# A hybrid decoder layer on one NeuronCore: 8192 bytes of DMA scratch in place of 16384, longer buffers for split weights, and one set of weights 64 bytes into them

## The chip, the core and the metric

The kernel runs on one core of a Trainium2 chip. The core has a matrix engine (TensorE, PE in the profile), a vector engine (VectorE, DVE), an engine for activation functions (ScalarE, ACT), a general one (GpSimd, POOL) and a synchronizing one (SyncE, SP), which here only issues transfers. Each engine works through its own instructions in order; engines wait for one another by semaphores. Sixteen DMA engines move data between HBM and SBUF, the on-chip memory of 128 partitions. TensorE accumulates in PSUM, eight banks of 512 float32 per partition.

The metric is the device time of one execution in microseconds: the median of several, each on the chip.

## What is computed

One layer of a decoder for a prompt of 512 tokens and for eight samples of eight tokens each (64 tokens), which share the weights. The reference computes in float32; the parts that matter here, shortened:

```python
u = _rms(x) * g_pre_mix
proj = u @ w_in
z, xbc, dt_raw, q, k, v, ig, fg, og = jnp.split(proj, split_at, axis=-1)
xbc, conv_new = causal_conv(xbc, conv_buf, conv_w, conv_b)
...
y_ssd, h_new = ssd_scan(xs, dt, a, bm, cm, h_ssm)
...
h_ml, c_new, n_new, m_new = mlstm_scan(q, k, v, i_pre, logf, mc, mn, mm)
...
x = x + _rms(jnp.concatenate([y_ssd, h_ml], axis=-1) @ w_out) * g_post_mix
...
o = (attention of (u @ w_xq) over memory keys and values) @ w_xo
x = x + _rms(o) * g_post_x
u = _rms(x) * g_pre_ffn
x = x + _rms((jax.nn.silu(u @ w_gate) * (u @ w_up)) @ w_down) * g_post_ffn
```

The mixer is the first half: an SSD scan (Mamba-2) and an mLSTM side by side, both in chunks. `v` above are the mixer's values, the 1024 columns of `w_in` that the change is about.

## The kernel before

**Products in three parts.** A float32 product is made of three products of rounded numbers (type float32r): a weight `w` is split into `whi`, its rounding, and `wlo`, the rounded rest; an activation likewise into `uh` and `ul`. Then `whi*uh + whi*ul + wlo*uh` is accumulated in one PSUM bank (`gemm`, lines L202, L203 and L205). In most products the weights are the stationary operand, 128x128, and the activations move past them, 256, 288 or 320 columns at a time.

**Weights.** `split_w` loads 128 x 1024 weights into a buffer `raw` by SP's queue, casts them to `whi` on ScalarE (L180), and makes `wlo` by a subtraction on VectorE or GpSimd (L187). With `acc=True` part of `wlo` is made otherwise: ScalarE writes `-whi` (L184) and GpSimd issues a transfer that adds the weights from HBM onto it (L185). In the FFN the class `Seven` does the same for the tiles of its seven products (`low`, L1796 and L1797), and `cast` reads a part of the weights' `lo` back from HBM (L1557). All these transfers are issued by GpSimd; the others by SP, a few by ScalarE. The tags `whi` and `wlo` of the pool `weights` have three buffers each, which every stage of the kernel shares: `split_w`, the first two tiles `wi`, `cast`, and `high1`, `parts2` and `place3` of `Seven`.

**The mixer's values** (`values`, L801 on) are the other way round: for each of two halves `g` of the heads, four units of weights are the moving operand, 512 columns at a time, and the activations of a chunk of tokens are stationary (L815). They come by `split_w` with `cut=1024`, the whole of `wlo` on VectorE. Each product is placed behind a step of the SSD of the prompt (the list `steps_`), so that TensorE works on values while the SSD's chain runs on the other engines.

**Where tiles lie.** At the bottom of SBUF lies the scratch of the dynamic transfers. Behind it come the pools in the order of their creation: constants, `weights`, `newton`, `big` (large activations), and on top of these the pools of the single stages as a stack. Pools with `side="right"` are taken from the upper end downwards: `ssds` (the SSD of the samples, L681), `mls` (the mLSTM of the samples, L941), `big0` (L1035) and others. With `reuse_waits="tile"` a tile waits only for those earlier tiles whose bytes it takes. A tile of a right-hand pool can so wait for a tile of the stack on the left, where both reach the same bytes at different times.

**What sets the order.** The program is built with `schedule_with_timeline_sim=True`: outside of parts that are ordered by hand, a list scheduler with reckoned times sets the order on each engine when the program is built. Hand-written constraints (`issue_after`) bind it: `behind` and `split_behind` hold the projection's tiles of `z` back until given steps of the SSD (L1026), `steps_` the values. The FFN and the end of the attention are ordered by hand.

**Around the SSD's end.** For each pair of heads `ssd_prompt` builds decays in the tiles `lm` and `ec` and adds the part that comes from earlier chunks on GpSimd (L659, named `xs<-xs,ec` in the profile). Then the samples' mLSTM begins: `ds_` (L951 to L957), `qpad`, cleared on GpSimd (L959) and filled by eight products (L961), and `kws` (L967); then for each of eight batch elements its products L981 and L988 on TensorE. Its last products (L936) stand ahead of the output projection of the mixer (`out1`).

Of the kernel before, what the change touches and what calls it, by code (L numbers as in the profile page):

```python
# [12 lines left out]
F32R = mybir.dt.float32r  # L13
# [6 lines left out]
P = 128  # L20
# [87 lines left out]
CUT = 512  # L108
# [3 lines left out]
NWX = 3  # L112
# [3 lines left out]
def build(nc, tc, ctx, I, O):  # L116
# [4 lines left out]
    wp = ctx.enter_context(tc.tile_pool(name="weights", bufs=1))  # L121
# [14 lines left out]
    def GP(name="g"):  # L136
        return pg.tile([P, 512], F32, name=name, tag="g")
# [31 lines left out]

    loads, casts = [], []  # L170

    def split_w(src, n=1024, cut=CUT, acc=False, pool=None, to=None, raw=None):
        if raw is None:
            raw = wp.tile([P, 1024], F32, name="raw", tag="raw", bufs=2)
        loads.append(S.dma_start(raw[:, :n], src))
        if to:
            split(*to, raw[:, :n])
            return to
        hi, lo = [(pool or wp).tile([P, 1024], F32R, name=k, tag=k, bufs=NWX if pool else 3) for k in ("whi", "wlo")]
        casts.append(A.copy(hi[:, :n], raw[:, :n]))  # L180
        for e, a, b in ((V, 0, cut), (G, cut, n)):
            if b > a and e is G and acc:

                A.activation(lo[:, a:b], hi[:, a:b].bitcast(F32), AF.Copy, scale=-1.0)  # L184
                G.dma_start(lo[:, a:b], src[:, a:b], accum_op=ALU.add)  # L185
            elif b > a:
                e.tensor_tensor(lo[:, a:b], raw[:, a:b], hi[:, a:b].bitcast(F32), op=ALU.subtract)  # L187
        return hi, lo

    def split(hi, lo, src, eng=None, cast=None):  # L190
        c = (cast or A.copy)(hi, src)  # L191
        (eng or V).tensor_tensor(lo, src, hi.bitcast(F32), op=ALU.subtract)  # L192
        return c
# [109 lines left out]
        mm(psw[:, 0:256], wz[:, 0:128], wz, start=True, stop=True, skip_group_check=True)  # L303
    S.dma_start(par, I["par"])

    wi = [[wp.tile([P, 1024], F32R, name=k, tag=k, bufs=3) for k in ("whi", "wlo")] for _ in range(2)]
    raws = [wp.tile([P, 1024], F32, name="raw", tag="raw", bufs=2) for _ in range(2)]
    for k in range(KT):
        if k % 2 == 0:
# [32 lines left out]
    with tc.issue_after(uhk.ins), tc.issue_after(ulk.ins):  # L342
        w2 = split_w(I["win"][3], cut=1024, raw=sp.tile([P, 1024], F32, name="raw2"))
# [19 lines left out]
    with tc.issue_after(last[0].ins), tc.issue_after(last[1].ins):  # L363
        w3 = split_w(I["win"][4], cut=1024)
# [8 lines left out]
    def in_tile(i, evac, cut=CUT):  # L373

        if i < 5:
            for (t0, n), ps in zip(HALVES, ps0[i - 1]):
                if ps is None:
                    ps = GP("ps_in")[:, :n]
                    with tc.issue_after(rows[-1].ins):
                        gemm(ps, [(*w3, KT)], U, UL, t0, n)  # L380
                evac(t0, n, xs[:, 5 + i, t0:t0 + n] if i < 3 else ps)
        else:
            with tc.issue_after(pows[0].ins), tc.issue_after(rops[0].ins):
                with ExitStack() as after:
                    for m in split_behind.get(i, ()):
                        after.enter_context(tc.issue_after(m.ins))
                    w = split_w(I["win"][i], cut=cut, acc=True)
            if i in behind:
                gemm2([(*w, KT)], U, UL, evac, "ps_in", [0])
            with tc.issue_after(behind[i].ins) if i in behind else ExitStack():  # L390
                gemm2([(*w, KT)], U, UL, evac, "ps_in", [1] if i in behind else [0, 1])
# [310 lines left out]
    for g in range(2):  # L702
        for hb in range(2):
            dst = cpad[:, g, 4 * hb:4 * hb + 4, :].rearrange("p b t -> p (b t)")
            src = bc[:, 2 + g, TP + 32 * hb:TP + 32 * hb + 32]
# [4 lines left out]
    for g in range(2):  # L710
# [13 lines left out]
        for h in range(8):  # L724
            k, j = h % 2, (8 * g + h) // 2
# [75 lines left out]
    def values(g):  # L801


        units, banks = {}, {}

        def unit(u):
            units[u] = split_w(I["wv"][g][:, u, :], cut=1024)

        def product(ps, a, b, **kw):

            while steps_[0][0] <= done[0]:
                steps_.append(steps_.pop(0))
            done[0] += 1
            with tc.issue_after(steps_[-1][1].ins):
                mm(ps, a, b, skip_group_check=True, **kw)  # L815

        def products(u, c, first, last):
            (hi, lo), (t0, n) = units[u], CHUNKS[c]
            if first:
                banks[c] = GP("ps_v")  # L820
            ps = banks[c]
            for i in range(2):
                k, w = 2 * u + i, slice(512 * i, 512 * i + 512)
                s_, e_ = first and i == 0, last and i == 1
                if n == TS:

                    product(ps, U(k, t0, P), hi[:, w], start=s_, stop=e_)
                    product(ps[:n], U(k, t0, n), lo[:, w], start=False, stop=e_)
                else:
                    product(ps, U(k, t0, n), hi[:, w], start=s_, stop=False)  # L830
                    product(ps, UL(k, t0, n), hi[:, w], start=False, stop=False)
                    product(ps, U(k, t0, n), lo[:, w], start=False, stop=e_)
            if not last:
                return
            p2 = ps.rearrange("p (h k) -> p h k", h=2)
            if n == TS:
                o = vts[:TS, 2 * g:2 * g + 2, 0:256]
                A.copy(o, p2[TS:P])
                V.tensor_tensor(o, o, p2[:TS], op=ALU.add)
                A.activation(o, o, AF.Copy, scale=rx[:TS, 4:5])  # L840
            else:
                A.activation(vt4[:, c, 2 * g:2 * g + 2, 0:256], p2, AF.Copy, scale=rx[:, c:c + 1])

        for u in range(4):
            with tc.issue_after(added[0].ins) if g == 0 and u < 2 else ExitStack():
                unit(u)
            for c in range(3):
                products(u, c, u == 0, u == 3)
        for u in (1, 2, 3, 0):
            for c in (3, 4):  # L850
                products(u, c, u == 1, u == 0)
            if u == 1:
                unit(0)
# [35 lines left out]
    for h in range(4):  # L889
        q, k = qk[:, h, :], qk[:, 4 + h, :]  # L890
# [657 lines left out]

    def cast(key, src, low, pool=None):

        hi, lo = [(pool or wp).tile([P, 1024], F32R, name=k, tag=k, bufs=NWX if pool else 3) for k in ("whi", "wlo")]
        A.copy(hi, W[key])
        if low is None:
            A.activation(lo, W[key], AF.Copy, scale=-1.0)
            G.dma_start(lo, src, accum_op=ALU.add)
        else:
            G.dma_start(lo, pre[:, low, :])  # L1557
        W[key] = hi, lo
# [160 lines left out]
    for n_, (key, p) in enumerate(order):  # L1719
        src = I[{"xo": "wxo", "g": "wgate", "u": "wup"}[key[0]]][key[1]]  # L1720
        at_(order[n_ - 2][1] + 0.01 if n_ > 1 else -1, load, key, src)
        if key[1] == 3:
            at_(p, cast3, n_)
            at_((0.55, 1.05)[n_], low3, n_)
        else:
            at_(p, cast, key, src, PRE.index(key) if key in PRE else None, wx if key in (("g", 0), ("u", 0), ("g", 1)) else None)
# [43 lines left out]
    class Seven:  # L1770
# [26 lines left out]
                G.dma_start(out, src, accum_op=ALU.add)  # L1797

        def high1(s):
            s.h1 = wp.tile([P, 1024], F32R, name="whi", tag="whi", bufs=3)  # L1800
            s.c1 = A.copy(s.h1[:, s.all], s.r1[:, s.all])  # L1801

        def sums(s):
# [1 line left out]
            V.tensor_tensor(sw[:, s.LA], sw[:, s.LB], s.r1[:, s.LA], op=ALU.subtract)  # L1805

        def parts2(s):
            s.h2, s.l2 = [wp.tile([P, 1024], F32R, name=k, tag=k, bufs=3) for k in ("whi", "wlo")]
            split(s.h2[:, s.all], s.l2[:, s.all], sw[:, s.all])

        def diffs(s):
# [3 lines left out]
            V.tensor_tensor(s.d4[:, 0:s.n], s.r1[:, s.LB], sw[:, s.LA], op=ALU.subtract)  # L1815

        def place3(s):
            s.h3, s.l3 = [wp.tile([P, 1024], F32R, name=k, tag=k, bufs=3) for k in ("whi", "wlo")]
            s.low(s.l3[:, s.LA], s.r2[:, s.LB], s.src2[:, s.LB], s.made[1])

        def parts3(s):
# [524 lines left out]

# [10 lines left out]
```

## Time and profile before

| | us |
|---|---|
| median of three runs | 1094.43 (1092.6 to 1095.0) |
| the profiled execution, whole | 1092.51 |
| its span in the trace | 1090.7 |
| TensorE busy | 1081.4 |
| VectorE busy | 753.3 |
| ScalarE busy | 611.6 |
| GpSimd busy | 227.0 |

The mean granted clock of TensorE was 0.997 of full speed. In the profile, L12 is line 12 of the kernel. A row such as `L185 POOL DMA_DIRECT2D wlo<-win x32 | 27.9, 871 | 80.0 <-...` is a group of 32 instructions of line 185 on GpSimd that took 27.9 us in all and 871 ns each; the engine had been idle for 80.0 us just before them, and what follows the arrow ended that. A row of a timeline gives start, duration, engine, line, operation, tiles and count, and in brackets the idle time before it with its releaser. TensorE overlaps a matmul with the next, so the durations of single matmuls add up to more than the time they take. A queue row gives packets, megabytes and the share of 16 DMA engines' time.

### The profile page before, as it was taken

To read this page: it belongs to the slowest core of one execution; us is meant where nothing else is said; L and a number is where in the kernel's file an instruction comes from. 1 tells how busy PE (TensorE), PEld (TensorE's weight loads), DVE (VectorE), ACT (ScalarE), POOL (GpSimd) and SP (SyncE) were. 2 spreads that over 40 slices of the span, in tenths; PEclk is the share of its full clock that TensorE was granted. 3 is DMA by queue.
4 is the path that set the end of the run, shared out by engine and by line. 5 is a ranking of instruction groups with operands and counts; after the bars stand their busy time and mean duration, and the time that the engine had idled before them with its cause. 6 is when DMAs were issued, how large, how long until landed. Compare 5 with 4: busy or idle time off the path is not lost.

```text
span 1090.7 us, 20715 instructions
## 1 busy us (share of the span) xinstructions
PE 1081.4 (99%) x8124; PEld 1024.5 (94%) x8124; DVE 753.3 (69%) x1507; ACT 611.6 (56%) x1098; POOL 227.0 (21%) x305
## 2 busy tenths in 40 slices
PE   9999999999999999999999999999999999999997
PEld 8999887778999999999988879999999999999997
DVE  6896775758877775568644556666567887787555
ACT  7867622355654555656544445645567566656653
POOL 1332643313213111000144301100011121111000
PEclk9999999999999999999999999999999999999999
DMA  6785635435655448653467865644476687578532
GB/s 209 181 156 126 161 114 168 164 86 177 190 150 145 108 138 292 218 193 110 144 219 277 270 238 175 217 153 103 116 184 146 150 197 175 116 186 187 128 130 88
DMA packets 58966, 182.29 MB, mean 167 GB/s; under 512 B 6604, under 2 KB 11852, under 8 KB 58356
## 3 DMA queue, kind: packets, MB, share of 16 engines
q1 hardware_dynamic: 42740, 138.06, 38.7%
q0 software_dynamic: 15552, 41.95, 19.6%
q8 instruction: 64, 1.05, 0.4%
q10 hardware_dynamic: 576, 0.95, 0.2%
q14 instruction: 34, 0.28, 0.1%
HBM read 160.28 MB, written 20.65 MB: 166 GB/s over the span
## 4 chain that ended last, share of the span: by engine, by line
PE 90%; DVE 4%; DMA 2%; issue 2%; ACT 2%; POOL 0%; SPq 0%; DVEq 0%; ACTq 0%; POOLq 0%
PE ps_in L203 5%; PE ps_in L202 5%; PE ps_in L205 5%; PE ps_v L815 3%; PE ps_o L205 3%; PE ps_o L203 3%; PE ps_o L202 3%; PE ps_u L1850 3%; PE ps_g L1850 3%; PE ps_g L1849 3%; PE ps_u L1851 3%; PE ps_g L1851 3%; PE ps_u L1849 3%; PE ps_dn L1849 2%; PE ps_dn L1851 2%; PE ps_dn L1850 2%
## 5 line engine op out<-in xcount | busy, mean ns | idle before, releaser
L202 PE MATMUL ps_in<-uh,whi 128*128 128x320 f32 (+1 forms) x544 | 163.3, 300 | 0.1
L205 PE MATMUL ps_in<-uh,wlo 128*128 128x320 f32 (+1 forms) x544 | 162.7, 299 | 0.2 <-DMA wlo<-win 0.2
L203 PE MATMUL ps_in<-ul,whi 128*128 128x320 f32 (+1 forms) x544 | 162.2, 298 | 0.0
L180 ACT CAST whi<-raw 128x1024 fp32r<-128x1024 f32 (+1 forms) x104 | 105.2, 1013 | 95.6 <-PE ps_in L203 25.9
L187 DVE TENSOR_TENSOR wlo<-raw,whi 128x512 fp32r<-128x512 f32 (+1 forms) x96 | 96.3, 1005 | 66.6 <-ACT whi L180 65.9
L202 PEld LDWEIGHTS ps_in<-uh,whi 128*128 128x128 f32 x544 | 102.9, 189 | 3.0 <-issue 1.7
L205 PEld LDWEIGHTS ps_in<-uh,wlo 128*128 128x128 f32 x544 | 102.7, 189 | 1.4 <-DMA wlo<-win 0.4
L203 PEld LDWEIGHTS ps_in<-ul,whi 128*128 128x128 f32 x544 | 102.9, 189 | 0.6
L185 POOL DMA_DIRECT2D wlo<-win x32 | 27.9, 871 | 80.0 <-ACT wlo L184 70.2
L1850 PE MATMUL ps_g<-b,whi 128*128 128x288 f32 x144 | 42.5, 295 | 0.0
L1850 PE MATMUL ps_u<-b,whi 128*128 128x288 f32 x144 | 42.5, 296 | 0.0
L1849 PE MATMUL ps_g<-b,whi 128*128 128x288 f32 x144 | 42.4, 295 | 0.0
L1849 PE MATMUL ps_u<-b,whi 128*128 128x288 f32 x144 | 42.2, 294 | 0.0
L1822 ACT CAST whi<-rawx 128x1024 fp32r<-128x1024 f32 (+1 forms) x26 | 25.6, 985 | 27.8 <-PE ps_dn L1850 13.8
L192 DVE TENSOR_TENSOR wlo<-sw,whi 128x1024 fp32r<-128x1024 f32 (+1 forms) x26 | 29.6, 1140 | 14.9 <-ACT whi L191 14.8
L202 PE MATMUL ps_xo<-qh,whi 128*128 128x288 f32 x128 | 38.6, 302 | 0.2 <-ACT whi L180 0.2
L205 PE MATMUL ps_o<-mixm_h,wlo 128*128 128x256 f32 (+1 forms) x128 | 37.8, 296 | 0.0
L202 PE MATMUL ps_o<-mixs_h,whi 128*128 128x320 f32 (+1 forms) x128 | 37.7, 295 | 0.0
L202 PE MATMUL ps_xq<-u2h,whi 128*128 128x320 f32 (+1 forms) x128 | 37.7, 299 | 0.0
L1801 ACT CAST whi<-raw 128x1024 fp32r<-128x1024 f32 (+1 forms) x26 | 25.6, 984 | 21.6 <-PE ps_g L1850 9.6
L203 PE MATMUL ps_o<-mixm_l,whi 128*128 128x256 f32 (+1 forms) x128 | 37.7, 294 | 0.0
L203 PE MATMUL ps_xo<-ql,whi 128*128 128x288 f32 x128 | 37.6, 295 | 0.0
(765 smaller groups left out, 3848.6 us busy)
## 6 DMA issues: line engine op xcount, KB each, us to landing
raw<-win SPq DMA_DIRECT2D x35, 512.0 KB, 4.1
raw<-wout SPq DMA_DIRECT2D x17, 512.0 KB, 3.6
raw<-wxq SPq DMA_DIRECT2D x13, 512.0 KB, 3.6
raw<-wgate SPq DMA_DIRECT2D x13, 512.0 KB, 3.7
raw<-wup SPq DMA_DIRECT2D x13, 512.0 KB, 4.8
wlo<-win POOLq DMA_DIRECT2D x24, 256.0 KB, 5.1
kva<-kc SPq DMA_DIRECT2D x12, 512.0 KB, 5.8
kva<-vc SPq DMA_DIRECT2D x12, 512.0 KB, 6.5
```

The costliest lines, as they stand in the source:

```text
L180: casts.append(A.copy(hi[:, :n], raw[:, :n]))
L185: G.dma_start(lo[:, a:b], src[:, a:b], accum_op=ALU.add)
L187: e.tensor_tensor(lo[:, a:b], raw[:, a:b], hi[:, a:b].bitcast(F32), op=ALU.subtract)
L192: (eng or V).tensor_tensor(lo, src, hi.bitcast(F32), op=ALU.subtract)
L202: mm(ps, wh, ah, start=i == 0, stop=False)
L203: mm(ps, wh, al, start=False, stop=False)
L205: m = mm(ps, tiles[order[c]][1], xh(order[c], t0, n), start=False, stop=c == len(tiles) - 1)
L815: mm(ps, a, b, skip_group_check=True, **kw)
L1801: s.c1 = A.copy(s.h1[:, s.all], s.r1[:, s.all])
L1849: mm(ps, wh, b[0][k], start=start and k == 0, stop=False, skip_group_check=True)
L1850: mm(ps, wh, b[1][k], start=False, stop=False, skip_group_check=True)
L1851: m = mm(ps, wl, b[0][k], start=False, stop=k == nk - 1, skip_group_check=True)
```

## The change

Three edits. `kernel` asks for 8192 bytes per partition of scratch for dynamic transfers; before it took the default, 16384. A new helper `half_w` gives the buffers of split weights out: 1088 columns (4352 bytes) instead of 1024 (4096), of which the 1024 from column `o` on are used; every user of the tags `whi` and `wlo` of the pool `weights` takes its buffer from it. The mixer's values pass `o=16`, so their weights start 16 columns, 64 bytes, into the buffers; all others start at 0. `split_w` hands `o` on.

```diff
--- before.py
+++ after.py
@@ -169,14 +169,17 @@
 
     loads, casts = [], []
 
-    def split_w(src, n=1024, cut=CUT, acc=False, pool=None, to=None, raw=None):
+    def half_w(k, o=0):
+        return wp.tile([P, 1088], F32R, name=k, tag=k, bufs=3)[:, o:o + 1024]
+
+    def split_w(src, n=1024, cut=CUT, acc=False, pool=None, to=None, raw=None, o=0):
         if raw is None:
             raw = wp.tile([P, 1024], F32, name="raw", tag="raw", bufs=2)
         loads.append(S.dma_start(raw[:, :n], src))
         if to:
             split(*to, raw[:, :n])
             return to
-        hi, lo = [(pool or wp).tile([P, 1024], F32R, name=k, tag=k, bufs=NWX if pool else 3) for k in ("whi", "wlo")]
+        hi, lo = [pool.tile([P, 1024], F32R, name=k, tag=k, bufs=NWX) if pool else half_w(k, o) for k in ("whi", "wlo")]
         casts.append(A.copy(hi[:, :n], raw[:, :n]))
         for e, a, b in ((V, 0, cut), (G, cut, n)):
             if b > a and e is G and acc:
@@ -303,7 +306,7 @@
         mm(psw[:, 0:256], wz[:, 0:128], wz, start=True, stop=True, skip_group_check=True)
     S.dma_start(par, I["par"])
 
-    wi = [[wp.tile([P, 1024], F32R, name=k, tag=k, bufs=3) for k in ("whi", "wlo")] for _ in range(2)]
+    wi = [[half_w(k) for k in ("whi", "wlo")] for _ in range(2)]
     raws = [wp.tile([P, 1024], F32, name="raw", tag="raw", bufs=2) for _ in range(2)]
     for k in range(KT):
         if k % 2 == 0:
@@ -804,7 +807,7 @@
         units, banks = {}, {}
 
         def unit(u):
-            units[u] = split_w(I["wv"][g][:, u, :], cut=1024)
+            units[u] = split_w(I["wv"][g][:, u, :], cut=1024, o=16)
 
         def product(ps, a, b, **kw):
 
@@ -1548,7 +1551,7 @@
 
     def cast(key, src, low, pool=None):
 
-        hi, lo = [(pool or wp).tile([P, 1024], F32R, name=k, tag=k, bufs=NWX if pool else 3) for k in ("whi", "wlo")]
+        hi, lo = [pool.tile([P, 1024], F32R, name=k, tag=k, bufs=NWX) if pool else half_w(k) for k in ("whi", "wlo")]
         A.copy(hi, W[key])
         if low is None:
             A.activation(lo, W[key], AF.Copy, scale=-1.0)
@@ -1797,7 +1800,7 @@
                 G.dma_start(out, src, accum_op=ALU.add)
 
         def high1(s):
-            s.h1 = wp.tile([P, 1024], F32R, name="whi", tag="whi", bufs=3)
+            s.h1 = half_w("whi")
             s.c1 = A.copy(s.h1[:, s.all], s.r1[:, s.all])
 
         def sums(s):
@@ -1805,7 +1808,7 @@
             V.tensor_tensor(sw[:, s.LA], sw[:, s.LB], s.r1[:, s.LA], op=ALU.subtract)
 
         def parts2(s):
-            s.h2, s.l2 = [wp.tile([P, 1024], F32R, name=k, tag=k, bufs=3) for k in ("whi", "wlo")]
+            s.h2, s.l2 = [half_w(k) for k in ("whi", "wlo")]
             split(s.h2[:, s.all], s.l2[:, s.all], sw[:, s.all])
 
         def diffs(s):
@@ -1815,7 +1818,7 @@
             V.tensor_tensor(s.d4[:, 0:s.n], s.r1[:, s.LB], sw[:, s.LA], op=ALU.subtract)
 
         def place3(s):
-            s.h3, s.l3 = [wp.tile([P, 1024], F32R, name=k, tag=k, bufs=3) for k in ("whi", "wlo")]
+            s.h3, s.l3 = [half_w(k) for k in ("whi", "wlo")]
             s.low(s.l3[:, s.LA], s.r2[:, s.LB], s.src2[:, s.LB], s.made[1])
 
         def parts3(s):
@@ -2346,7 +2349,7 @@
 
 def kernel(**inputs):
     arrays = pack(inputs)
-    nc = bacc.Bacc("TRN2", target_bir_lowering=False, num_devices=1)
+    nc = bacc.Bacc("TRN2", target_bir_lowering=False, num_devices=1, dynamic_dma_scratch_size=8192)
     I = {k: nc.dram_tensor(k, v.shape, mybir.dt.from_np(v.dtype), kind="ExternalInput").ap() for k, v in arrays.items()}
     O = {k: nc.dram_tensor("o_" + k, s, F32, kind="ExternalOutput").ap() for k, s in OUTS.items()}
     with tile.TileContext(nc, **TCOPT) as tc:
```

## The prediction

> **What bounds the kernel now.** I read the page first, then the waits of TensorE, then the busy time of each engine by stage.
>
> ```profile
> PE 1081.4 (99%) x8124; PEld 1024.5 (94%) x8124; DVE 753.3 (69%) x1507; ACT 611.6 (56%) x1098; POOL 227.0 (21%) x305
> ...
> q0 software_dynamic: 15552, 41.95, 19.6%
> ...
> PE 90%; DVE 4%; DMA 2%; issue 2%; ACT 2%; POOL 0%; SPq 0%; DVEq 0%; ACTq 0%; POOLq 0%
> ```
>
> TensorE is busy for 1081.4 of 1090.7 us and holds 90% of the chain that ended last; what is left is mostly the start and the last stores. The waits of TensorE by releaser say the same:
>
> ```profile
> PE ps_warm L303 <- DVE wz L300: 1.1, 1, 1.1
> PE ps_ct L554 <- ACT r L533: 0.3, 1, 0.3
> PE ps_in L205 <- DMA wlo<-win: 0.2, 1, 0.2
> PE ps_xo L202 <- ACT whi L180: 0.2, 1, 0.2
> ```
>
> Four waits, 1.8 us in all. So the change can gain in three ways only: products that take less time, products that switch less between kinds, or one of these 0.2 us. It can lose wherever a transfer or another engine comes so late that TensorE has nothing to do. The places where that is near are those in which the change can alter the order of work, 206 to 264 us (columns: stretch, its length, then busy time of PE, PEld, DVE, ACT, POOL):
>
> ```profile
> 206.00:222.00 16.00, 16.00 (x88) 12.41 (x87) 11.65 (x20) 5.49 (x8) 1.93 (x1) 1.00 0.49 161
> 222.00:240.00 18.00, 18.00 (x99) 13.36 (x98) 7.94 (x20) 9.08 (x14) 3.37 (x4) 1.00 0.23 58
> 240.00:256.00 16.00, 15.76 (x137) 14.37 (x137) 12.38 (x30) 9.03 (x17) 4.15 (x7) 1.00 0.57 126
> 256.00:264.00 8.00, 8.00 (x63) 8.00 (x62) 7.94 (x18) 6.78 (x13) 6.41 (x13) 1.00 0.95 347
> ```
>
> TensorE is full there at a granted clock of 1.00, but from 256 to 264 us VectorE (7.94 of 8.00) and GpSimd (6.41) are full too.
>
> **The change part by part.** No instruction, byte or queue entry is added or taken out of the source. What changes is addresses, and through them which tile waits for which.
>
> **1. The values' weights, 64 bytes in.** These buffers are the moving operand of 224 products of 512 columns:
>
> ```profile
> L815 PE MATMUL ps_v<-whi,uh x80: 390/397/584, 167.0 to 239.6; 128*128 128x512 f32 x80
> ...
> L815 PE MATMUL ps_v<-wlo,uh x80: 387/394/582, 167.5 to 239.8; 128*128 128x512 f32 x64, 128*64 128x512 f32 x16
> ...
> L815 PE MATMUL ps_v<-whi,ul x64: 390/394/582, 167.3 to 238.5; 128*128 128x512 f32 x64
> ```
>
> Matmuls overlap, so a product's price is the distance from one start to the next, not its 394 ns:
>
> ```profile
> 174.51 0.39 PE L815 MATMUL ps_v<-wlo,uh 128*128 128x512 f32 x1
> ...
> 176.37 0.39 PE L815 MATMUL ps_v<-wlo,uh 128*128 128x512 f32 x1
> ```
>
> Eight intervals lie between these two: 1.86/8 = 232.5 ns each. Counting the tiles from the bottom of SBUF (16384 bytes of scratch, the constants, then the weights), each buffer of weights starts at 96 modulo 256 bytes now; 8192 less and 4352 in place of 4096 per buffer (both multiples of 256) leave that so, and only the values' weights go to 160. One other kind of product of this width has a moving operand that starts at 160 modulo 256, the attention's:
>
> ```profile
> 592.30 0.61 PE L1374 MATMUL ps_ov<-prh,mv 128*128 128x512 f32 x2
> 592.75 0.39 PE L1375 MATMUL ps_ov<-prl,mv 128*128 128x512 f32 x1
> ...
> 594.11 0.39 PE L1376 MATMUL ps_ov<-prh,mv 128*128 128x512 f32 x1
> ```
>
> From 592.30 to 594.11 there are again eight intervals (the first row holds two products): 226 ns. So the bounds are 0 and 224 x 6.5 ns = 1.5 us gained, if the phase of the address is the reason. The stationary operand and the accumulation differ between the two as well, so I take half, **-0.7 us**. Nothing hides it: TensorE is full in these rows' stretch.
>
> [...]
>
> The producers of these weights (the cast on ScalarE, the subtraction on VectorE, the load on SP's queue) keep their shapes, and none of the 1.8 us of waits lies on values, so they cost **0**.
>
> **2. Scratch halved.** [...] The queue's row has 15552 packets; they come from 108 issues (32 of L185, 52 of L1797, 24 for weights prepared ahead), 144 each. Issues by first and last start, with shortest, median and longest duration in ns:
>
> ```profile
> L185 POOL DMA_DIRECT2D wlo<-win x32 | 27.9, 871 | 80.0 <-ACT wlo L184 70.2
> ...
> L1797 POOL DMA_DIRECT2D wacc<-wgate x9: 850/850/932, 732.3 to 998.6; - x9
> ```
>
> The early issues take 871 ns on average, and the same kind between 732 and 999 us still 850. So with the large scratch an issue does not grow late in the run: no sign that space runs short. With half, the nearest row for a price is one more issue's length, 0.86 us, on the issues that come after the scratch is used up. What could be late is the transfer with the least room, in the FFN:
>
> ```profile
> 872.68 1.20 POOL L1797 DMA_DIRECT2D wlo<-wdown  x1
> ...
> wlo<-wdown POOLq DMA_DIRECT2D x8, 192.0 KB, 5.4
> ...
> 879.74 0.30 PE L1851 MATMUL ps_dn<-hh,wlo 128*128 128x288 f32 x1
> ```
>
> It is issued by 873.88, lands about 5.4 us on, 879.28, and TensorE wants it at 879.74: 0.46 us to spare. So 0.86 us more costs 0.4 us at this place, and there are two to six like it (eight such issues): 0.8 to 2.4 us. I take **0**, the lower end, since the flat 850 ns is the nearest row, and keep +2.4 for the range. Nothing can be gained here.
>
> [...]
>
> **3. Everything below moves.** The left side of SBUF starts 8192 bytes lower and its buffers of weights are 1536 bytes longer in all, so the tiles behind them sit 6656 bytes lower, while pools that allocate from the right stay. Two tiles of the samples' mLSTM, `qpad` and `ds_`, now share bytes with the prompt SSD's right-hand `lm` and `ec`; 6656 lower they don't. That takes away their wait for the last of the SSD. It shows in GpSimd's timeline:
>
> ```profile
> 222.00 1.01 POOL L659 TENSOR_TENSOR xs<-xs,ec 128x384 f32<-128x384 f32 x1 [14.08 <-DVE ec L657]
> 234.92 1.02 POOL L659 TENSOR_TENSOR xs<-xs,ec 128x384 f32<-128x384 f32 x1 [11.90 <-DVE ec L657]
> 236.98 0.88 POOL L185 DMA_DIRECT2D wlo<-win  x1 [1.03 <-ACT wlo L184]
> ...
> 255.22 1.00 POOL L659 TENSOR_TENSOR xs<-xs,ec 128x384 f32<-128x384 f32 x1 [0.45 <-DVE ec L657]
> 256.28 0.96 POOL L959 MEMSET qpad<- 128x1024 f32 x1
> ...
> 258.17 1.37 POOL L961 TENSOR_TENSOR qpad<-qk,vt 128x32 f32<-128x32 f32 x6
> 259.50 1.68 POOL L952 TENSOR_TENSOR ds__3156<-ds__3156,c 64x256 f32<-64x256 f32 x1
> 261.15 0.45 POOL L961 TENSOR_TENSOR qpad<-qk,vt 128x32 f32<-128x32 f32 x2
> ```
>
> The clearing of `qpad` starts right behind the last addition that reads `ec`, and this prologue (0.96 + 1.37 + 1.68 + 0.45 = 4.5 us) fills GpSimd where VectorE is full. Freed of the wait, the list scheduler, which fixes each engine's order when the program is built, may place it in the idle 14.08 or 11.90 us before the additions. Nothing on TensorE waits for the prologue today (no row in its waits), so an earlier one brings **0** by itself. It may change how the samples' products mix with the projection's, which has a price:
>
> ```profile
> 389.69 1.03 PE L936 MATMUL ps_ht<-c,num 128*128 128x128 f32 x8
> 390.49 0.37 PE L202 MATMUL ps_o<-mixs_h,whi 128*128 128x256 f32 x1
> 390.69 0.28 PE L203 MATMUL ps_o<-mixs_l,whi 128*128 128x256 f32 x1
> 390.81 0.27 PE L205 MATMUL ps_o<-mixs_h,wlo 128*128 128x256 f32 x1
> ```
>
> After plain products the first of the rounded ones takes 0.20 us to its successor, the next 0.12: 0.08 to 0.1 us for a switch. The mLSTM goes over 8 batch elements with some two switches each, so about 20 more or fewer are the most a new order makes: -2 to +2 us. With no reason for either sign I take **0**. An earlier prologue can also push work behind it; that is a rival.
>
> **Sum.** -0.7 + 0 + 0 = -0.7 us. The profiled execution took 1092.51 us, its span of 1090.7 and 1.8 around it; the sum against it gives 1091.8. The three runs (1092.6, 1094.43, 1095.0) have their median 1.9 us above it. The middle of all four is 1093.5, and **1092.8** follows. What a measurement of this kernel can tell from no change is about 0.2%, 2.2 us, the spread of the runs.
>
> **The rivals.**
>
> **Faster (1090.0).** The address is all of the 6.5 ns (-1.5), and the prologue, moved into GpSimd's idle 12 to 14 us, lets the scheduler join the samples' products into longer blocks (-2): 1093.5 - 3.5. For it: the idle stretches, and VectorE and GpSimd full from 256 to 264 us, a knot that would come undone. Against it: a full TensorE gains nothing from a knot elsewhere, and two other differences may explain the 6.5 ns.
>
> **Slower, a prologue in front of a load (1098.0).** GpSimd works in order. The issue at 236.98 is the very transfer for which TensorE waits 0.2 us already (`wlo<-win`), so it has no room. If the freed prologue is placed behind the addition at 234.92 and ahead of this issue, all of its 4.5 us appear on TensorE: 1093.5 + 4.5. It decides from the point where more than the 1.03 us of idle ahead of the issue is filled. Against it: the scheduler reckons times and has 11.90 us of room earlier; its inputs are there by 228 us, but its reckoned times need not be the chip's.
>
> **Slower, the scratch (1095.2).** As in step 2, with the upper end: 1092.8 + 2.4. For it: 108 issues through half the room. Against it: the duration that doesn't vary over the run.
>
> **It does nothing (1093.5).** The scheduler leaves the order as it is and the phase has no effect. It lies inside my forecast's own spread and is counted with it.
>
> **How the numbers follow.** Forecast 0.40, faster 0.33, prologue 0.15, scratch 0.12. A measured median scatters by some 1.2 us to either side (half of 1092.6 to 1095.0). Of the forecast's 0.40, 0.29 lies within 0.2%, 0.08 faster, 0.03 slower; of the 0.33, 0.30 faster and 0.03 the same; of the 0.15, 0.13 slower and 0.02 the same; of the 0.12, 0.07 slower, 0.03 the same, 0.02 faster. Together 0.40 faster, 0.37 the same, 0.23 slower. The likeliest case alone spans 1090.8 (-1.5, -1.2) to 1094.7. The range takes the rivals in: down to 1090.0 - 1.2 and 0.8 more for a new order, 1088; up to 1098.0 + 0.5, 1098.5. The prologue's case with the scratch's on top stays out.
>
> **What would show it.** Step 1: the distance of the ps_v products, 232.5 ns now, 229 by my sum, 226 at best. Step 2: mean durations of L185 and L1797 on GpSimd, 850 to 871 ns now, and a DMA wait on TensorE after 700 us if I am wrong. Step 3: the start of the clearing of `qpad`, 256.28 now, and TensorE's idle time between 220 and 264 us; over 1 us there is the slower rival. A changed distance of products with buffers that kept their phase (L202, L203, L205) would upset the whole working.

## The result, and the profile after

The changed kernel took 1109.22 us (1107.92 to 1110.56) against 1094.07 before (1092.6 to 1095.0): a ratio of 1.014, 95% interval 1.0121 to 1.0158. It is slower by some 15 us, outside the predicted range of 1088 to 1098.5.

The page of the changed kernel (its lines are numbered 3 higher from `split_w` on: L205, L206 and L208 are the three products, L188 the transfer that adds):

```profile
PE 1087.0 (98%) x8124; PEld 1027.7 (93%) x8124; DVE 752.8 (68%) x1507; ACT 611.5 (55%) x1098; POOL 227.9 (21%) x305
...
q0 software_dynamic: 15552, 41.95, 19.3%
...
PE 81%; DMA 7%; ACT 4%; DVE 4%; issue 3%; POOL 1%; SPq 0%; DVEq 0%; ACTq 0%; POOLq 0%
```

Counts and bytes are those of before, and the three other compute engines are as busy as they were. But TensorE's share of the chain fell from 90% to 81%, so it now waits. Its waits by releaser (total, times, longest, in us):

```profile
PE ps_ht L939 <- DVE num L935: 5.8, 1, 5.8
PE ps_in L208 <- DMA wlo<-win: 2.8, 1, 2.8
PE ps_o L205 <- ACT f_mix L1087: 1.9, 1, 1.9
PE ps_warm L306 <- DVE wz L303: 1.1, 1, 1.1
PE ps_o L208 <- DVE wlo L190: 0.9, 2, 0.7
```

With six more of 0.2 to 0.4 us, the waits come to 14.6 us, against 1.8 before. That is 12.8 of the 18.1 us by which the profiled span grew (1108.8 against 1090.7). The two longest answer to the two places where the order of work changed.

**At 58 us: a transfer is issued late.** GpSimd's timeline of the changed kernel:

```profile
51.34 2.25 POOL L710 COPY cpad<-bc 128x8 f32<-128x8 f32 x8
53.53 0.82 POOL L188 DMA_DIRECT2D wlo<-win  x1
...
54.30 5.78 POOL L710 COPY cpad<-bc 128x8 f32<-128x8 f32 x8
```

These copies fill `cpad`, a tile of the samples' SSD. Before, its clearing and copies ran from 106.7 to 112 us, as the tile's own rows show (before, then changed):

```profile
L701 POOL MEMSET cpad<- x1: 862/862/862, 106.7 to 106.7; 128x512 f32 x1
```

```profile
L704 POOL MEMSET cpad<- x1: 521/521/521, 1.4 to 1.4; 128x512 f32 x1
```

GpSimd works in order, so the issue that came at 50.24 us before (first row below, from the timeline of before) stands behind eight copies at 53.53 now. Its transfer also takes longer, 7.2 us from issue to landing in place of 5.1 (second fence, before and then changed), while eight more copies run on GpSimd behind it. So it lands 5.4 us later, 3.3 of them by the issue and 2.1 by the transfer; what lengthens the transfer was not tried. TensorE pays for it, in its own timeline (third fence) and in the busy time by stretch (fourth; length, then PE, PEld, DVE, ACT, POOL, and the granted clock before the last two):

```profile
50.24 0.77 POOL L185 DMA_DIRECT2D wlo<-win  x1
```

```profile
wlo<-win POOLq DMA_DIRECT2D x1, 512.0 KB, 5.1
...
wlo<-win POOLq DMA_DIRECT2D x1, 512.0 KB, 7.2
```

```profile
57.66 0.28 PE L206 MATMUL ps_in<-ul,whi 128*128 128x256 f32 x1
60.76 0.58 PE L208 MATMUL ps_in<-uh,wlo 128*128 128x256 f32 x1 [2.83 <-DMA wlo<-win]
```

```profile
57.90:60.70 2.80, 0.03 (x1) 0.00 (x0) 2.80 (x6) 2.37 (x5) 2.80 (x8) 0.98 0.97 193
60.70:64.10 3.40, 3.33 (x16) 3.34 (x17) 0.88 (x2) 0.87 (x2) 2.31 (x7) 0.51 0.84 200
```

After 2.83 us of nothing come 3.4 us at a granted clock of 0.51. Some 16 products start in them, 0.21 us apart where 0.12 us is usual, so this costs about another 1.5 us.

**At 400 us: the last head of the prompt's mLSTM is late.** The samples' mLSTM starts its prologue at 219.9 us, 36.4 us earlier than before (256.28):

```profile
L962 POOL MEMSET qpad<- x1: 960/960/960, 219.9 to 219.9; 128x1024 f32 x1
```

What it passes comes later. First the SSD's products L644 and the prompt heads' scores L903 of before (first and last start at the end of the row's middle part), then the same two lines of the changed kernel, L647 and L906:

```profile
L644 PE MATMUL ps_yi<-lm,xdt x128: 272/273/323, 138.8 to 253.2; 128*64 128x128 f32 x128
...
L903 PE MATMUL ps_s<-qk x32: 271/275/275, 254.5 to 355.4; 128*128 128x128 f32 x32
```

```profile
L647 PE MATMUL ps_yi<-lm,xdt x128: 272/273/324, 143.1 to 260.9; 128*64 128x128 f32 x128
...
L906 PE MATMUL ps_s<-qk x32: 270/275/377, 262.5 to 370.4; 128*128 128x128 f32 x32
```

The first SSD product is 4.3 us late (that is the loss at 58 us, still there), the last one 7.7, the first head 8.0, the last head 15.0. Four heads follow one another, and each one's steps on VectorE and ScalarE share these engines with the samples'. At the end TensorE has used up the projection's products that filled the time:

```profile
394.50 0.30 PE L208 MATMUL ps_in<-uh,wlo 128*128 128x320 f32 x1
400.57 1.33 PE L939 MATMUL ps_ht<-c,num 128*128 128x128 f32 x5 [5.77 <-DVE num L935]
```

```profile
394.80:400.60 5.80, 0.03 (x2) 0.03 (x1) 4.20 (x16) 1.35 (x3) 1.04 (x1) 0.82 0.66 180
400.60:404.00 3.40, 3.40 (x16) 3.40 (x17) 1.72 (x7) 1.64 (x4) 0.00 (x0) 0.50 0.00 1
404.00:406.00 2.00, 2.00 (x14) 2.00 (x13) 2.00 (x5) 1.94 (x5) 0.00 (x0) 0.66 0.00 0
```

5.77 us of idle time, then half the clock until about 405.4 us (the 0.66 of the last row is the mean of a part at half and a part at full clock). Before, this same product stood at 389.69 with no wait at all, while the last step on `num` began at 389.4:

```profile
L932 DVE TENSOR_SCALAR num<-num,hn_a x16: 345/350/354, 284.9 to 389.4; 128x256 f32<-128x256 f32 x16
```

There was no room, and nothing in the list of waits says so.

**What did not go wrong.** The values' products became faster as forecast, and a GpSimd issue late in the run is as long as ever (`wacc<-wgate`, shortest, median, longest, first and last start):

```profile
178.48 0.39 PE L818 MATMUL ps_v<-whi,ul 128*128 128x512 f32 x1
...
180.55 0.39 PE L818 MATMUL ps_v<-wlo,uh 128*128 128x512 f32 x1
```

```profile
L1800 POOL DMA_DIRECT2D wacc<-wgate x9: 860/862/930, 751.0 to 1016.7; - x9
```

Nine intervals lie between the two rows of products: 230 ns each. Over all products of the values that follow one another, the mean distance is 229.9 ns in the changed trace and 233.2 in that of before.

### The profile page after: what moved, and what is told of

It is laid out like the page before. It is cut to its first block, busy times and chain, and to the rows that moved or that the text cites. A ratio compares the mean times of both kernels' runs of the same rounds, so it can differ in the third digit from the quotient of the medians.

```text
span 1108.8 us, 20715 instructions
## 1 busy us (share of the span) xinstructions
PE 1087.0 (98%) x8124; PEld 1027.7 (93%) x8124; DVE 752.8 (68%) x1507; ACT 611.5 (55%) x1098; POOL 227.9 (21%) x305
## 4 chain that ended last, share of the span: by engine, by line
PE 81%; DMA 7%; ACT 4%; DVE 4%; issue 3%; POOL 1%; SPq 0%; DVEq 0%; ACTq 0%; POOLq 0%
PE ps_in L205 5%; PE ps_in L208 5%; PE ps_v L818 5%; PE ps_in L206 5%; PE ps_u L1853 3%; PE ps_g L1853 3%; PE ps_g L1852 3%; PE ps_u L1854 3%; PE ps_g L1854 3%; PE ps_u L1852 3%; PE ps_dn L1852 2%; PE ps_dn L1854 2%; PE ps_dn L1853 2%; PE ps_dn L205 2%; PE ps_dn L208 2%
## 5 line engine op out<-in xcount | busy, mean ns | idle before, releaser
L208 PE MATMUL ps_in<-uh,wlo 128*128 128x320 f32 (+1 forms) x544 | 162.7, 299 | 2.8 <-DMA wlo<-win 2.8
L205 PE MATMUL ps_in<-uh,whi 128*128 128x320 f32 (+1 forms) x544 | 164.4, 302 | 0.5 <-DVE cb L454 0.4
L183 ACT CAST whi<-raw 128x1024 fp32r<-128x1024 f32 (+1 forms) x104 | 105.2, 1013 | 106.8 <-PE ps_in L206 27.9
L206 PE MATMUL ps_in<-ul,whi 128*128 128x320 f32 (+1 forms) x544 | 163.0, 300 | 0.0
L190 DVE TENSOR_TENSOR wlo<-raw,whi 128x512 fp32r<-128x512 f32 (+1 forms) x96 | 96.6, 1008 | 77.1 <-ACT whi L183 76.3
L208 PEld LDWEIGHTS ps_in<-uh,wlo 128*128 128x128 f32 x544 | 102.7, 189 | 5.1 <-DMA wlo<-win 3.0
L205 PEld LDWEIGHTS ps_in<-uh,whi 128*128 128x128 f32 x544 | 102.9, 189 | 3.0 <-DVE cb L454 0.6
L206 PEld LDWEIGHTS ps_in<-ul,whi 128*128 128x128 f32 x544 | 102.9, 189 | 1.5 <-issue 0.8
L188 POOL DMA_DIRECT2D wlo<-win x32 | 29.1, 910 | 98.8 <-ACT wlo L187 85.8
L205 PE MATMUL ps_o<-mixs_h,whi 128*128 128x320 f32 (+1 forms) x128 | 38.7, 302 | 1.9 <-ACT f_mix L1087 1.9
L208 PE MATMUL ps_o<-mixm_h,wlo 128*128 128x256 f32 (+1 forms) x128 | 38.1, 298 | 0.9 <-DVE wlo L190 0.9
L205 PE MATMUL ps_xo<-qh,whi 128*128 128x288 f32 x128 | 38.6, 302 | 0.2 <-ACT whi L183 0.2
L206 PE MATMUL ps_o<-mixs_l,whi 128*128 128x320 f32 (+1 forms) x128 | 38.2, 299 | 0.0
L208 PE MATMUL ps_o<-mixs_h,wlo 128*128 128x320 f32 (+1 forms) x128 | 38.2, 298 | 0.0
L205 PE MATMUL ps_xq<-u2h,whi 128*128 128x320 f32 (+1 forms) x128 | 37.7, 299 | 0.0
L205 PE MATMUL ps_o<-mixm_h,whi 128*128 128x256 f32 (+1 forms) x128 | 37.7, 295 | 0.0
```

Of the source, the lines that this page charges most:

```text
L205: mm(ps, wh, ah, start=i == 0, stop=False)
L206: mm(ps, wh, al, start=False, stop=False)
L208: m = mm(ps, tiles[order[c]][1], xh(order[c], t0, n), start=False, stop=c == len(tiles) - 1)
```

## The experiments

My theory: the loss is in the order of work alone. A right-hand pool that no longer reaches into the left stack comes free early, and the scheduler starts its work as soon as its inputs are there. Two rivals: the smaller scratch makes transfers late (scratch), or the longer, shifted buffers slow something down (buffers). All kernels from here on keep the line numbers of before.

**e1, e2, e3: the order alone.** In the changed kernel, one unused tile of 6656 bytes is reserved as the first of the samples' SSD pool, of the samples' mLSTM pool, or of both. No instruction touches it and every other tile stays where the change put it; the two pools only reach as far into the left stack again as before.

```diff
     sd = st2.enter_context(tc.tile_pool(name="ssds", bufs=1, side="right", reuse_waits="tile"))
+    sd.tile([P, 1664], F32, name="gap")      # e1, e3
...
     ms = st2.enter_context(tc.tile_pool(name="mls", bufs=1, side="right", reuse_waits="tile"))
+    ms.tile([P, 1664], F32, name="gap")      # e1, e2
```

> The changed kernel, all of its tiles at its own addresses, with one unused reservation of 6656 bytes as the first tile of each of the two right-hand pools (samples' SSD, samples' mLSTM), which reach again into the left-hand stack as before the change. Nothing is computed otherwise. Theory 'order' (pools that no longer reach into the left stack let the scheduler start the samples' work early, in front of loads and of the prompt's mLSTM): all of the loss goes, 1093.4 us (before less 0.7 us for the values' products). Rival 'scratch' (half the scratch makes GpSimd's transfers late): it stays at 1109. Rival 'buffers' (longer buffers or the 64 bytes slow products or their producers): it stays at 1109.

> The changed kernel with the unused reservation in the samples' mLSTM pool alone; the samples' SSD still starts early. Theory 'order': the wait of 5.8 us for the last of the prompt's mLSTM (num of L935) goes, and with it some 12 us; the wait of 2.8 us for a transfer at 58 us with the low clock behind it stays: 1093.4 + 3.1 = 1096.5 us. Rivals 'scratch' and 'buffers': 1109.

> The changed kernel with the unused reservation in the samples' SSD pool alone; the samples' mLSTM still starts early. Theory 'order': only the wait at 58 us goes, 1109.2 - 3.1 = 1106.1 us. Rivals 'scratch' and 'buffers': 1109.

Measured: e1 1092.9 us (ratio to before 0.9993, 0.9985 to 1.0002); e2 1094.96 (1.0016, 1.0008 to 1.0025); e3 1104.02 (1.0098, 1.0084 to 1.0111), with the kernel before at 1093.35 beside them. The waits of e2 and of e3, the first row of each:

```profile
PE ps_in L205 <- DMA wlo<-win: 3.0, 2, 2.8
```

```profile
PE ps_ht L936 <- DVE num L932: 5.8, 1, 5.8
```

Each reservation takes away just the wait that belongs to its pool. With both, GpSimd's early copies are gone and the issue stands where it stood before:

```profile
50.58 0.76 POOL L185 DMA_DIRECT2D wlo<-win  x1
```

So the scratch of 8192 bytes, the longer buffers and the 64 bytes are all there in e1, and none of the loss is. In the programs as they were built, the instructions of each of the five engines stand in e1 in the order of the kernel before. The early SSD costs 2.1 us (e2 less e1; 3.1 expected), the early mLSTM 11.1 (e3 less e1). e2 and e3 lie 1.5 and 2.1 us below what I expected; both expectations used the 3.1 us, and that of e3 started from the first measured time, 1109.2.

**e4: the scratch halved, nothing else.**

```diff
-    nc = bacc.Bacc("TRN2", target_bir_lowering=False, num_devices=1)
+    nc = bacc.Bacc("TRN2", target_bir_lowering=False, num_devices=1, dynamic_dma_scratch_size=8192)
```

> The kernel before with the scratch halved and nothing else: buffers of 4096 bytes, values' weights at their start. The left stack lies 8192 bytes lower instead of 6656. Theory 'order': the order of work is the changed kernel's, so the loss is all there, and the 0.7 us of the values' products are missing: 1109.9 us. Rival 'scratch': 1109 as well. Rival 'buffers': 1094.

Measured: 1106.34 us (1.0116, 1.0101 to 1.0132). The loss is there without the buffers, so the rival 'buffers' falls. The order of every engine's instructions is the changed kernel's. The size was 3.6 us below what I expected, which made me measure the changed kernel once more.

**e5: the changed kernel again.**

> The changed kernel again, beside the next three. Theory 'order' with parts that add up: holding the samples' SSD gave back 2.1 us where the mLSTM was held too, so 1104.0 + 2.1 = 1106.1. If the two early starts feed on one another beyond their sum, it stays at the first measurement, 1109.

Measured: 1106.39 us (1.0114, 1.0099 to 1.0129). The two early starts add up: 2.1 + 11.1 = 13.2, and 1106.4 - 1092.9 = 13.5. The first measurement's ratio, 1.014, is 2.6 thousandths higher, nearly 3 us, and its fastest execution (1107.92) is slower than the slowest of e5 (1107.34). The two traces differ in places: at 58 us the first one runs 3.4 us at half the clock (0.51) behind a wait of 2.83 us, where e5 runs at full clock (1.00 from 60.6 to 64 us) behind 2.69 us but waits another 1.2 us for the next transfer; and the first one waits twice for weights of the output projection (the row `ps_o L208 <- DVE wlo L190` above), which e5 does not. Why the whole of the first measurement is slower stays open.

**e6, e9: which of the samples' mLSTM's early pieces cost.** From e3 (SSD held), e6 puts the products of the samples' mLSTM behind the last SSD product on TensorE; e9 puts `ds_` on VectorE, the clearing of `qpad` on GpSimd and the transposes for `kws` on TensorE back too.

```diff
+ with tc.issue_after(inner[7].ins):     # e6, e9
     mm(psn[32 * h:32 * h + 32, 0:257], ds_[r, h, r], ...)
     mm(psn[32 * h:32 * h + 32, 0:257], qpad[:, h, bb, :], ...)
     mm(ps[:, 0:258], km[:, h * P:(h + 1) * P], ...)
...
+ with tc.issue_after(mults[15].ins):    # e9
     V.tensor_tensor(ds_, pb3[:TS], ...)
+ with tc.issue_after(adds[7].ins):      # e9, adds: the additions of ec on GpSimd
     G.memset(qpad, 0.0)
+ with tc.issue_after(inner[7].ins):     # e9
     TE.transpose(psk[:TS, h * P:(h + 1) * P], ...)
```

> The kernel with the samples' SSD held (1104.0) in which the samples' mLSTM keeps its early prologue (ds_, qpad, kws on VectorE, GpSimd, ScalarE), but its products on TensorE (L974, L981, L988) are put behind the prompt SSD's last product of L644. Sub-theory 'products': the early products and the updates of states that hang on them stand ahead of the SSD's last pair of heads and delay it by 3.4 us and the prompt's mLSTM behind it: the loss goes, 1093 to 1096 us. Sub-theory 'prologue': the early pieces on GpSimd and VectorE do it: it stays at 1104.

> As e6 (samples' SSD held, products of the samples' mLSTM behind the prompt SSD, 1098.35 us), and now its pieces on GpSimd and VectorE too: qpad's clearing behind the last addition of ec, ds_ behind the last lm, the transposes of kws behind the last product of L644. Free to come early are then only its loads of states on SP's queue and the stacks of the values on ScalarE and VectorE. Sub-theory 'engines in order': what e6 left over, 5.4 us against e1, is GpSimd's and VectorE's pieces, and the time comes to 1093 to 1094.5. Sub-theory 'loads': SP's early loads of states stand ahead of the projection's weights and cost the rest: it stays at 1096 to 1098.

Measured: e6 1098.35 us (1.0042, 1.0027 to 1.0057), e9 1096.09 (1.0024, 1.0015 to 1.0034). Neither sub-theory of e6 holds by itself: moving the products gives back 5.7 of the 11.1 us, and the wait for `num` is gone from its waits. The pieces that e9 adds give back another 2.3. That leaves 3.2 us, e9 less e1. SP's queues of e1 and of e9 differ just where 'loads' would have it:

```profile
218.06 35.04 SPq L175 DMA_DIRECT2D raw<-win  x6
253.19 2.84 SPq L979 DMA_DIRECT2D c<-c  x4
```

```profile
213.85 4.25 SPq L979 DMA_DIRECT2D c<-c  x4
220.17 35.51 SPq L175 DMA_DIRECT2D raw<-win  x6
```

**e13: the loads of states alone.** From e1, the states' buffers get a pool of their own.

```diff
+    c0s = st2.enter_context(tc.tile_pool(name="states", bufs=1, side="right", reuse_waits="tile"))
     ms = st2.enter_context(tc.tile_pool(name="mls", bufs=1, side="right", reuse_waits="tile"))
...
-            c0 = ms.tile([P, 4, 258], F32, name="c0", tag="t4", bufs=4)
+            c0 = c0s.tile([P, 4, 258], F32, name="c0", tag="t4", bufs=4)
```

> As e1 (both pools held, 1092.9 us), but the four buffers for the states of the samples' mLSTM get a pool of their own without a reservation, so that their first four loads stand on SP's queue ahead of six loads of the projection's weights, as in e9; every other engine keeps e1's order. Sub-theory 'loads': the 3.2 us between e9 and e1 are theirs, 1096 us. If not: 1093, and the 3.2 us belong to what e9 still starts early on ScalarE and VectorE (stacks of the values, m4t) and to the order that follows from it.

Measured: 1092.76 us (0.9993, 0.9985 to 1.0002). Early loads cost nothing in the order of e1, and 'loads' falls. By elimination the 3.2 us of e9 lie with what it still starts early on ScalarE and VectorE and with the order that follows, which in e9 differs from e1's on TensorE as well; no run shows it directly, and which of these pieces it is stays open.

**e7: the order by hand, no reservation.** Four places of the changed kernel get a constraint (the expectation counts five).

```diff
+ with tc.issue_after(ends_[0].ins): G.memset(cpad, 0.0)     # ends_: the products xe on GpSimd
+ with tc.issue_after(mults[15].ins): V.tensor_tensor(ds_, ...)
+ with tc.issue_after(adds[7].ins): G.memset(qpad, 0.0)
+ with tc.issue_after(inner[7].ins): TE.transpose(psk, ...)
```

> The changed kernel with no reservation and five constraints on order instead: cpad's clearing behind the first xe on GpSimd, ds_ behind the last lm on VectorE, qpad's clearing behind the last addition of ec on GpSimd, the transposes of kws behind the last product of L644. Theory 'order': 1093 to 1095 us, all tiles and weights where the changed kernel has them. Rivals 'scratch' and 'buffers': 1109.

Measured: 1096.53 us (1.0027, 1.0018 to 1.0037), with no wait of TensorE above 1.1 us. It takes back some 10 us of the loss as e5 has it, so both rivals fall once more, but it misses the 1095 at most that I expected. The stacks of the values, which are still free, come early (at 246.0 us in place of 254.8 in e1), as in e9; that the rest of the loss is theirs is not shown. A reservation holds a whole pool; constraints hold what they name.

**e8, e10, e11, e12: the phase of the moving operand.** The starting address of a moving operand modulo 256 bytes: 96 for the values' weights before, 160 after, 160 for most activations. All four build on e1. e8 gives each of the values' four units its own phase; the others move the large activations, and in e11 and e12 the values' weights as well.

```diff
-  units[u] = split_w(I["wv"][g][:, u, :], cut=1024, o=16)
+  units[u] = split_w(I["wv"][g][:, u, :], cut=1024, o=16 * u)   # e8; e11 o=40, e12 o=24
...
   nv = ctx.enter_context(tc.tile_pool(name="newton", bufs=1))
+  nv.tile([P, 48], F32, name="gap0")                            # e10; e11 24, e12 8 columns
```

> As e1 (both held, 1092.9 us), with the values' weights of unit u at 64 x u bytes into their buffer, so that the four units have their moving operand at 96, 160, 224 and 32 modulo 256. If the distance of ps_v products hangs on that phase: near 233 ns for unit 0 and 230 for unit 1 as measured so far, with 226 to 236 for the other two, and the time within 1.5 us of 1092.9. If the 3.3 ns come from something else than the phase (say from buffers that no longer follow at a distance of 4096 bytes): 230 for all four, and 1092.9.

> As e1 (1092.9 us), with the large activations and all tiles behind them 192 bytes higher, so that the moving operands of the projections, attention and FFN start at 96 modulo 256 in place of 160, the phase at which the values' products took 233.2 ns in place of 229.9. If the phase acts on every product alike, by the same 1.4%: some 5000 products of 256 to 320 columns take about 2 ns more, 1092.9 + 10 = 1103 us. If it acts on the values' products alone (512 columns, weights as the moving operand): 1093, with ps_in at 117.5 and 146.7 ns as before.

> As e1 (1092.9 us), with the large activations 96 bytes higher and the values' weights 160 bytes into their buffers: the moving operands of 1616 products of 256 columns and of the 224 values' products start at 0 modulo 256. e10 showed 119.4 ns at 96 against 117.5 ns at 160 for 256 columns, and e8 for 512 columns 232.9 at 96, 230.6 at 160, 231.0 at 224, 232.1 at 32. If the distance follows the phase smoothly, 0 lies between 224 and 32: 231.5 ns and some 118.3 ns, so 1092.9 + 0.4 + 1.3 = 1094.6 us. If an operand that starts on a boundary of 256 bytes is read fastest: below 117.5 and 229.9 ns, and 1090 to 1092.

> As e11, with 32 bytes for the activations and 96 for the values' weights: phase 192, between the two best so far. Smooth in the phase: at or slightly below 117.5 and 229.9 ns, 1092.5 us, a version at least as fast as e1. If only 160 itself is good: 118 to 119.4 and 231 to 233 ns, 1094 to 1095.

Measured: e8 1093.55 us (0.9996, 0.9987 to 1.0006), e10 1094.84 (1.0014, 1.0005 to 1.0024), e11 1095.57 (1.0017, 1.0008 to 1.0026), e12 1096.02 (1.0021, 1.0012 to 1.003). Mean distance from one product's start to the next of the same stage, by phase (ns, from the starts in the traces, without the intervals that other work or a wait lengthens):

| phase modulo 256 | 512 columns, ps_v | 256 columns, ps_in | 320 columns, ps_in |
|---|---|---|---|
| 96 | 233.2 (before), 232.9 (e8) | 119.5 (e10) | 146.8 (e10) |
| 160 | 229.9 (e1), 230.6 (e8) | 117.6 (e1) | 146.6 (e1) |
| 224 | 231.0 (e8) | | |
| 32 | 232.1 (e8) | | |
| 0 | 230.1 (e11) | 118.4 (e11) | 146.8 (e11) |
| 192 | 230.3 (e12) | 119.3 (e12) | 147.0 (e12) |

The 3.3 ns of the values' products come from the phase: in e8 the buffers are the longer ones, and unit 0 at phase 96 is back at 232.9. Products of 256 columns feel it too (119.5 ns at 96 against 117.6 at 160; an estimate of 1.9 ns times some 1600 of them is 3 us, and e10 lost 1.9 against e1), those of 320 hardly (146.6 to 147.0); neither forecast of e10 had that. It is not smooth: 192 lies between the two best phases for 512 columns and is bad for 256. For e11 the smooth forecast held at 256 columns (118.3 expected) and missed at 512 (231.5 expected) and the time by 1 us; for e12 the smooth forecast missed everywhere, and the other one held at 256 columns alone. The distances do not account for the times to the last us: e11 took longer than e10 with shorter distances. 160, where the activations lay already, stays the best tried. No kernel here beats the one before beyond its interval; e1 and e13 are the nearest.

## Why the prediction was wrong

**Step 3 failed: "Freed of the wait, the list scheduler ... may place it in the idle 14.08 or 11.90 us before the additions", priced at 0, with -2 to +2 us for another mix of products.** The mechanism was named, and the price was wrong. I reckoned the prologue alone, 4.5 us on GpSimd, against GpSimd's idle time. What came free was the whole of the samples' mLSTM with its products and updates. The prologue did land in the idle stretch (219.9 us), and everything behind it moved up with it and shared TensorE, VectorE and ScalarE with the prompt's SSD and mLSTM: 11.1 us, of which the products are 5.7, the pieces on GpSimd and VectorE 2.3, the loads nothing, and 3.2 are not pinned to a piece. The sign that the prediction had named, idle time of TensorE between 220 and 264 us, stayed away: the loss came out at 58 and 400 us.

**The rest of that step overlooked a pool.** It looked for tiles that share bytes, and found `qpad` and `ds_` (it calls `lm` and `ec` right-hand; their pool `ssd` belongs to the stack on the left). The samples' SSD came free too, because its first tile `xdts` no longer lay on the convolution's `ac`. `cpad` shared bytes with nothing on the left before or after; it had waited behind its pool's first tile. e1 to e3 show the rule at work: there no tile that is used moves, an unused one ahead of it waits, and the whole pool waits with it. "No row in its waits" was the second error of the step. That nothing waits for the samples' work says nothing of what waits behind it, and the prompt's last head had no room at 389.69 us.

**The slower rival was right in kind.** "A prologue in front of a load": GpSimd in order, a load behind it, its whole delay on TensorE. It came about at another load, at 58 us, by `cpad`, and cost 2.1 us; at the issue of 236.98 us, where I put it, the changed kernel lost nothing. (In e6 TensorE does wait there, for 1.2 us in place of 0.2.) The larger part was not a load at all. With 1098.0 us as its price and 0.15 as its chance, this rival was both too small and too unlikely.

**Step 1 was right in sign and cause, and its size was luck:** 233.2 to 229.9 ns, 224 x 3.3 = 0.74 us against 0.7 forecast, and by the phase, as e8 shows. But the half of 6.5 ns was a choice between two bounds with no row behind it; the other 3.9 ns that set the attention's products (226) apart from these have another reason, which no run looked for.

**Step 2 was right:** an issue late in the run takes 862 ns with half the scratch (850 before; 847 in e1, which has the small scratch and the old order), TensorE waits for no transfer after 700 us, and e1 is at the time of before. That the scratch bears on GpSimd's issues, and that they could use it up, was assumed there; no run shows either.

**The faster rival fell with step 3:** its undone knot was the loss.

## What to carry to other kernels

In a program whose order a scheduler chooses, addresses are part of the order: a size changed in one pool can take away a wait between two others, and a wait that goes is not a gain when the engine that counts was never waiting for it. Before a layout is changed, list the first tile of each pool against what lies under it, and treat each such overlap as a constraint that holds the whole pool; where the order is good, write it down as a constraint of its own. A product with no wait in the profile may still have no room: compare its start with the end of what it needs.

## What was unexpected in the hardware

Idle time of TensorE cost more than itself at two places of the changed kernel. Behind 5.77 us of it came some 4.8 us at half the clock (0.50 from 400.6 to 405 us); behind 2.83 us came 3.4 us at 0.51, but behind 2.77 us in e2 and 2.69 us in e5 full clock (1.00 from 60.6 to 64 us in both). In the trace of before, a low clock (0.54 from 80.0 to 83.7 us) came without any gap over 0.32 us, behind 2.4 us of small products (100 x 100 and 4 x 4) with TensorE busy for 2.08 of them:

```profile
76.90:79.30 2.40, 2.08 (x13) 1.34 (x11) 2.34 (x5) 2.34 (x5) 0.43 (x2) 1.00 0.74 203
79.30:80.00 0.70, 0.70 (x6) 0.68 (x7) 0.70 (x2) 0.68 (x2) 0.00 (x0) 1.00 1.13 228
80.00:83.70 3.70, 3.70 (x19) 3.70 (x18) 3.54 (x8) 3.65 (x6) 1.19 (x5) 0.54 0.79 187
```

In the trace of e1, which has the same order of work, the same products stand in the same stretch, and the clock stays full (1.00) behind them:

```profile
76.90:79.30 2.40, 2.09 (x13) 1.44 (x12) 2.34 (x5) 2.34 (x5) 0.44 (x2) 1.00 0.43 44
...
80.00:83.70 3.70, 3.70 (x30) 3.70 (x29) 3.54 (x8) 3.65 (x6) 1.04 (x3) 1.00 0.98 251
```

So the low clock came in one execution and not in another: with the same order of work, the trace of before has it here and that of e1 doesn't. In it 19 products run in place of 30, which is 11 x 0.12 = 1.3 us. Two single traces can differ by that much with the same order of work.

What sets the low clock off was not shown; the stretch of before shows that an idle TensorE is not needed.

The other is the phase: where in 256 bytes a moving operand of 256 or 512 columns starts changed the distance between products by up to 1.6% in these traces (119.5 against 117.6 ns, 233.2 against 229.9), and at 320 columns by 0.3% at most (146.6 to 147.0). Why was not settled.
